# A two-layer hybrid transformer block: the second attention's work follows a written plan instead of a rule

## The chip, the cores and the metric

The kernel runs on one NeuronCore of a Trainium2 chip, as one launch. The metric is device time in microseconds (us). TensorE (PE) does the matmuls; VectorE (DVE), ScalarE (ACT) and GpSimd (POOL) do the rest of the arithmetic; SyncE (SP) issues almost all DMAs, in the order of its queue.

## The reference, cut to what matters

Two layers on 512 tokens of width 1024. The first layer's attention mixes two kinds of head; the second's has 16 heads of one kind ("moba"), and it is the one that is changed here. After each attention stands a gated feed-forward network.

```
proj = h @ w_in_odd[i]                       # h = rmsnorm(x), 512 x 1024
mq, mk, mv = jnp.split(proj, 3, axis=-1)     # 16 heads of 64 each
mq = apply_partial_rope(mq.reshape(B, S, N_MOBA_HEADS, HEAD_DIM), cos, sin)
mk = apply_partial_rope(mk.reshape(B, S, N_MOBA_HEADS, HEAD_DIM), cos, sin)
moba_out = moba_attention(mq, mk, mv)        # blocks of 256 keys, the best 3 earlier blocks and the own one
x = x + moba_out.reshape(B, S, N_MOBA_HEADS * HEAD_DIM) @ w_out_odd[i]
x = x + conv_glu_ffn(rmsnorm(x, ffn_norm[layer]), ...)
```

With 512 tokens there are two blocks, so every earlier block is always selected and the attention is plain causal attention; the kernel computes it so.

## The kernel before

All matmuls are of single-precision numbers split into a high and a low part, so a product takes three matmuls (`mm3`: high by high, low by high, high by low). A `chunk` is 128x1024 weights: SP loads it (`raw`), ACT casts its high part (`wh`), DVE subtracts the low part (`wl`). There are three buffers each of raw, wh and wl, so SP's load of a chunk waits for the `wl` of the chunk three before it, and the cast waits until PE has used the chunk three before.

The second attention handles its 16 heads as 8 pairs, p = 0 to 7, and one piece of work is one of these:

- k (`ks`): `proj` (24 matmuls of 512 columns into one of three PSUM banks "mm"), `rope` (DVE shuffle and product, POOL product, DVE sum), `halves` (ACT high part, DVE low part), and `stack_k`: six moves of 64 partitions by DMA, because the two heads of a pair need their halves at other partitions. The last two, `mk_h<-mk_h` and `mk_l<-mk_l`, wait for the moves before them.
- q (`qs`): the same with `stack_q`: `mq_a<-mq_h` and `mq_a<-mq_l` for the first head (e = 0), then `mq_l<-mq_h` for the second head (e = 1). All moves go through SP's queue, between the weight loads.
- v (`vals`): the values of two pairs at once, two chunks, 96 matmuls of 256 columns into two "mm" banks.
- s (`soft`): the scores and softmax of one head. Eight matmuls (two for each block of 128 queries) go through two PSUM banks "S" (`s_m`), DVE adds the mask and takes the maximum (`prt_m`, L348), ACT takes the exponential, POOL scales. There are two `prt` buffers.
- m (`mix`): ten transposes of the probabilities on PE (`t_m`, two banks "T"), ACT and DVE split them (`pt_m_0h`, `pt_m_0l`, ..., and `p3`, which the trace calls p), eight matmuls by the values (`o_m`) into the single bank "O", and an ACT copy (L383) and a DVE sum (L384) that empty it into `y`.
- o (`out_proj`): a quarter of the output projection for the first four pairs.

The order in which the pieces are written comes from `heads`: the scores of a head, then an equal share of the work due for the next pair, then the value products of the head before. The order inside each engine's queue is then set by the framework's scheduler, which takes the written order as priority and moves an instruction back while it takes its inputs or buffers to be not ready. No engine reorders at run time: an instruction that waits holds up all behind it on its engine.

Before any `rope` of this attention can finish, `moba_scale` must have run: it makes the row scale of the norm (`rstd_of`: four transposes `st_n`, a DVE reduction, a dozen small DVE instructions, four transposes `bc_n`) and scales the two rope tables (`CR`, `SR`). Before, it was called inside the first `v_group`, the first piece.

Of the kernel before, what the change touches and what calls it, by code (L numbers as in the profile page):

```python
# [46 lines left out]

N_BIG, N_V, N_TMP, N_COL, N_PR, N_W = 25, 2, 7, 8, 2, 3
N_PSUM = {"mm": 3, "S": 2, "T": 2, "O": 1}


def _pieces(c, bits):
# [19 lines left out]
def hybrid_kernel(ctx: ExitStack, tc: tile.TileContext, xT_d, pos_d, const_d, vec_d, w_d, out_d, idx):  # L72
    nc = tc.nc
    V, A, G, PE = nc.vector, nc.scalar, nc.gpsimd, nc.tensor
# [13 lines left out]
    def tmp(name):  # L88
        return tp.tile([P, T], F32, tag="tmp", name=name, bufs=N_TMP)
# [146 lines left out]
    def halves(y, nm, eng=V):  # L236
        h, l = big(f"{nm}_h"), big(f"{nm}_l")
        split(h, l, y, eng)
        return h, l
# [284 lines left out]
                done(2 * p + e, Q[1])  # L524
        last(Q[1])

    def heads(pairs, work):


        work = list(work)  # L530
        prev = None

        def finish(pr):
            p, e, probs = pr
            c = pairs[p]
            mix(f"{c['nm']}{e}", e, probs, values[c["v"]], c["hv"] + e, c["y"])
            if e == 1:
                c["out"].append(halves(c["y"], f"o_{c['nm']}", c.get("lo", V)))

        for p, c in enumerate(pairs):  # L540
            while work and work[0][0] <= p:
                work.pop(0)[1]()
            c["y"] = tmp(f"y_{c['nm']}")
            for e in range(2):
                probs = soft(f"{c['nm']}{e}", e, c["q"], c["k"], c["bias"], c["decay"][e] if "decay" in c else None)
                n = len([1 for w in work if w[0] <= p + 1])
                for _ in range((n + 1 - e) // (2 - e)):
                    work.pop(0)[1]()
                if prev is not None:
                    finish(prev)  # L550
                prev = (p, e, probs)
        finish(prev)
        for w in work:
            w[1]()

    values = {}

# [6 lines left out]
    w = chunk("misc", 512)  # L564
# [102 lines left out]
    def fox(p):  # L667
        def vals():
            values["f", p // 2] = v_group(f"fv{p // 2}_")

        def qs():
            c["q"] = stack_q(scaled(proj(f"fq{p}"), f"fq{p}"), f"fq{p}")

        def ks():
            c["k"] = stack_k(scaled(proj(f"fk{p}"), f"fk{p}"), f"fk{p}", G)

        c = {"nm": f"f{p}", "v": ("f", p // 2), "hv": 2 * (p % 2), "bias": causal, "out": fo, "lo": G,
             "decay": [(selr[:, P + h:P + h + 1], ck) for h in (2 * p, 2 * p + 1)]}
        return c, ([vals] if p % 2 == 0 else []) + [ks, qs]

    def dsa(p):
        def vals():
# [24 lines left out]
            c["k"] = stack_k(o, f"dk{p}")  # L707

        c = {"nm": f"d{p}", "v": ("d", p // 2), "hv": 2 * (p % 2), "bias": [causal[0]] + tmask[1:], "out": do}
        return c, [ks, qs] + ([vals] if p % 2 == 0 else [])  # L710

    pairs, work = [], []
    for n in range(8):
        c, w = (fox if n < 4 else dsa)(n % 4)
        pairs.append(c)
        if n == 0:
            w = [x for i, f in enumerate(w) for x in (f, lambda i=i: index_scores(i + 1))]
        elif n == 2:
            w.append(lambda: select(1, range(16)))
        elif n > 2 and n < 5:  # L720
            w[1:1] = [lambda n=n: select(n - 1, range(8))]
            w.append(lambda n=n: select(n - 1, range(8, 16)))
        work += [(n, f) for f in w]
        if n == 7:
            work.append((7, lambda: out_proj("oe0_", fo, part=[0])))
    work += [(8, lambda m=m: out_proj("oe0_", fo, part=[m])) for m in range(1, 4)]
    heads(pairs, work)
    acc = sq_acc(1)
    out_proj("oe1_", do, lambda d: prep(d, 1, acc))
    lo_on_pool = False  # L730
# [8 lines left out]


    def moba_scale():
        rstd_main(accs[2], "n2")
        rope_scaled()

    mo = ([], [])

    def moba(p):
        def vals():
            values["m", p // 2] = v_group(f"mv{p // 2}_", moba_scale if p == 0 else None)

        def qs():
            c["q"] = stack_q(rope(proj(f"mq{p}"), f"mq{p}"), f"mq{p}")

        def ks():
            c["k"] = stack_k(rope(proj(f"mk{p}"), f"mk{p}"), f"mk{p}")

        c = {"nm": f"m{p}", "v": ("m", p // 2), "hv": 2 * (p % 2), "bias": causal, "out": mo[p // 4]}
        return c, ([vals] if p % 2 == 0 else []) + [ks, qs]

    pairs, work = [], []  # L760
    for n in range(8):
        c, w = moba(n)
        pairs.append(c)
        work += [(n, f) for f in w]
        if n == 7:
            work.append((7, lambda: out_proj("oo0_", mo[0], part=[0])))
    work += [(8, lambda m=m: out_proj("oo0_", mo[0], part=[m])) for m in range(1, 4)]
    heads(pairs, work)
    accs[3] = sq_acc(3)
    out_proj("oo1_", mo[1], lambda d: prep(d, 3, accs[3]))  # L770
    fin = {}
# [153 lines left out]
```

## Time and profile before

| | |
|---|---|
| median of 3 runs | 1262.97 us (1261.54 to 1265.6) |
| the profiled execution, own time | 1261.51 us |
| its span, first to last instruction | 1259.7 us |
| mean granted TensorE clock | 0.993 |
| PE busy over the span | 1220.4 us, 97% |
| DVE, ACT, POOL busy | 810.9, 557.4, 357.7 us |
| the second attention in the trace | 637.11 to 885.68 us |

The stretch of the second attention begins with its first projection matmul and ends with the first matmul of the second feed-forward network. "Busy" is the union of an engine's instructions; a matmul's record is longer than its pace, so a stall shows first in the distance between two starts.

### The profile page before, as it was taken

The page shows a single profiled execution, that of the slowest core. Times are in us where ns is not written, and L with a number is a line of the kernel's source. Part 1 is how long each engine was busy: PE and PEld are TensorE (multiplying, and loading weights), DVE is VectorE, ACT ScalarE, POOL GpSimd, SP SyncE. Part 2 cuts the span into 40 slices and gives each one's busy share as a digit, 9 for nine tenths or more (in the row PEclk, how much of TensorE's full clock was granted, in tenths as well). Part 3 has the DMA queues.
Part 4 walks back from the last instruction along what each step waited for, and adds up shares of the span by engine and source line. Part 5 has one row for each costly group of instructions (what it writes and reads, how often), then busy time and mean ns, then how long its engine had stood idle before and what let it go on. Part 6 is the DMA issues. An engine that isn't in the chain of part 4 may idle for free.

```text
span 1259.7 us, 16807 instructions
## 1 busy us (share of the span) xinstructions
PE 1220.4 (97%) x5996; PEld 1018.3 (81%) x5996; DVE 810.9 (64%) x1489; ACT 557.4 (44%) x969; POOL 357.7 (28%) x394
## 2 busy tenths in 40 slices
PE   6889999999999999999999999999999999999997
PEld 4768778778888888888887888888888888888887
DVE  7889988675654555544666778787655555444555
ACT  5564667653332333333445556555433333332334
POOL 3665557542111111111213223332222111111110
PEclk9989999999999999999999999999999999999999
DMA  5333444222333322323325434331233332333321
GB/s 194 101 92 111 128 99 128 63 80 89 101 100 100 98 90 93 96 93 100 103 96 142 113 100 123 105 109 67 84 93 108 100 100 92 94 100 101 96 88 67
DMA packets 57379, 127.24 MB, mean 101 GB/s; under 512 B 7584, under 2 KB 21024, under 8 KB 57296
## 3 DMA queue, kind: packets, MB, share of 16 engines
q1 hardware_dynamic: 56368, 124.81, 33.2%
q10 hardware_dynamic: 864, 1.17, 0.3%
q8 instruction: 47, 0.77, 0.2%
q14 instruction: 36, 0.29, 0.1%
q0 software_dynamic: 64, 0.20, 0.0%
HBM read 104.13 MB, written 2.10 MB: 84 GB/s over the span
## 4 chain that ended last, share of the span: by engine, by line
PE 79%; DVE 10%; issue 5%; ACT 3%; DMA 2%; POOL 1%; POOLq 0%; ACTq 0%; DVEq 0%; SPq 0%
PE mm_g L160 6%; PE mm_g L161 6%; PE mm_g L159 6%; PE mm_u L161 6%; PE mm_u L159 6%; PE mm_u L160 6%; PE mm_d L161 6%; PE mm_d L160 6%; PE mm_d L159 6%; DVE tmask L630 2%; DVE m L629 1%; DMA mq_l<-mq_h 1%; PE t_m L372 1%; PE o_m L381 1%; PE mm_mk L160 1%
## 5 line engine op out<-in xcount | busy, mean ns | idle before, releaser
L434 POOL TENSOR_TENSOR cv<-cv,gs 128x512 f32<-128x512 f32 x44 | 57.1, 1298 | 546.2 <-ACT gs L433 546.2
L159 PE MATMUL mm_d<-a_h,wh_d 128*128 128x512 f32 (+1 forms) x384 | 142.8, 372 | 0.0
L160 PE MATMUL mm_d<-a_l,wh_d 128*128 128x512 f32 (+1 forms) x384 | 142.6, 371 | 0.0
L161 PE MATMUL mm_d<-a_h,wl_d 128*128 128x512 f32 (+1 forms) x384 | 142.6, 371 | 0.0
L503 DVE TENSOR_TENSOR us<-mm_u,cv 128x512 f32<-128x512 f32 x44 | 30.4, 692 | 168.1 <-PE mm_u L161 132.7
L160 PE MATMUL mm_g<-xl,wh_g 128*128 128x512 f32 x352 | 137.2, 390 | 0.4 <-DVE xl L175 0.4
L159 PE MATMUL mm_u<-xh,wh_u 128*128 128x512 f32 x352 | 137.3, 390 | 0.0
L161 PE MATMUL mm_u<-xh,wl_u 128*128 128x512 f32 x352 | 137.0, 389 | 0.0
L160 PE MATMUL mm_u<-xl,wh_u 128*128 128x512 f32 x352 | 137.0, 389 | 0.0
L161 PE MATMUL mm_g<-xh,wl_g 128*128 128x512 f32 x352 | 137.0, 389 | 0.0
L159 PE MATMUL mm_g<-xh,wh_g 128*128 128x512 f32 x352 | 137.0, 389 | 0.0
L148 ACT CAST wh_g<-raw_g 128x1024 fp32r<-128x1024 f32 x44 | 46.3, 1052 | 143.1 <-PE mm_g L160 141.6
L500 DVE TENSOR_TENSOR gs<-mm_g,RB 128x512 f32<-128x512 f32 x44 | 30.4, 691 | 118.2 <-PE mm_g L161 115.7
L128 ACT CAST wh_d<-raw_d 128x1024 fp32r<-128x1024 f32 x45 | 47.4, 1054 | 123.7 <-PE mm_u L160 103.4
L160 PEld LDWEIGHTS mm_d<-a_l,wh_d 128*128 128x128 f32 x384 | 72.3, 188 | 12.5
L159 PEld LDWEIGHTS mm_d<-a_h,wh_d 128*128 128x128 f32 x384 | 72.3, 188 | 12.5
L161 PEld LDWEIGHTS mm_d<-a_h,wl_d 128*128 128x128 f32 x384 | 72.3, 188 | 12.4
L160 PEld LDWEIGHTS mm_g<-xl,wh_g 128*128 128x128 f32 x352 | 66.1, 188 | 14.8 <-DVE xl L175 1.1
L161 PEld LDWEIGHTS mm_u<-xh,wl_u 128*128 128x128 f32 x352 | 66.1, 188 | 13.8
L159 PEld LDWEIGHTS mm_g<-xh,wh_g 128*128 128x128 f32 x352 | 66.1, 188 | 13.7
L161 PEld LDWEIGHTS mm_g<-xh,wl_g 128*128 128x128 f32 x352 | 66.1, 188 | 13.7
L160 PEld LDWEIGHTS mm_u<-xl,wh_u 128*128 128x128 f32 x352 | 66.1, 188 | 13.6
(778 smaller groups left out, 3072.4 us busy)
## 6 DMA issues: line engine op xcount, KB each, us to landing
raw_g<-in_w SPq DMA_DIRECT2D x44, 512.0 KB, 3.5
raw_u<-in_w SPq DMA_DIRECT2D x44, 512.0 KB, 3.6
raw_d<-in_w SPq DMA_DIRECT2D x41, 256.0 KB, 2.9
raw_d<-in_w SPq DMA_DIRECT2D x29, 192.0 KB, 2.6
raw_d<-in_w SPq DMA_DIRECT2D x34, 128.0 KB, 2.4
raw_oe<-in_w SPq DMA_DIRECT2D x8, 512.0 KB, 4.0
raw_mv<-in_w SPq DMA_DIRECT2D x8, 512.0 KB, 3.5
raw_mk<-in_w SPq DMA_DIRECT2D x8, 512.0 KB, 4.0
```

What stands on the lines that cost most here:

```text
L128: A.copy(dst_h, src)
L148: A.copy(wh, raw)
L159: PE.matmul(out, ah, bh, start=first, stop=False)
L160: PE.matmul(out, ah, bl, start=False, stop=False)
L161: PE.matmul(out, al, bh, start=False, stop=last)
L372: PE.transpose(t[:, n * P:n * P + P], probs[i][:, j * P:j * P + P], ident)
L381: PE.matmul(o[:, o0:o0 + w], vj, ph[:, c0:c0 + w], start=j == 0, stop=False)
L434: G.tensor_tensor(cv, cv, gs, op=OP.mult)
L500: V.tensor_tensor(gs, og, RB, op=OP.mult)
L503: V.tensor_tensor(us, ou, cv, op=OP.mult)
L629: V.max(m8, sc)
L630: V.match_replace(sc, m8, sc, -3e38)
```

## The change

`heads` is replaced by `attention`, which goes through a plan, a string of steps such as `k3` (keys of pair 3), `s10` (scores of pair 1, head 0) or `m10` (its value products). The first attention's plan, PLAN0, writes out the order that `heads` gave: on every engine the rows are the same as before up to the second attention. PLAN1 for the second attention is a different order. `moba_scale` now runs after the first projection of any kind, which is q of pair 1. No instruction is added or removed: PE has 5990 rows either way, DVE 1420, ACT 849, POOL 399, SP 461. Lines of the changed kernel stand 12 further down (L148 becomes L160).

```
+PLAN1 = (
+    "q1 q0 k0 k3 v0 s00 k1 q2 m00 k2 s01 s10 s11 q3 s20 q4 s21 m01 v2 m10 m11 k4 s30 s31 m20 m21 v4 k5 q6 "
+    "m30 q5 s40 m31 s41 m40 k6 s50 k7 s51 m41 v6 q7 o0 s60 s61 s70 m50 m51 s71 o1 m60 m61 o2 o3 m70 m71 "
+)
...
-    def heads(pairs, work):
...
-            c["y"] = tmp(f"y_{c['nm']}")
-            for e in range(2):
-                probs = soft(f"{c['nm']}{e}", e, c["q"], c["k"], c["bias"], c["decay"][e] if "decay" in c else None)
-                n = len([1 for w in work if w[0] <= p + 1])
-                for _ in range((n + 1 - e) // (2 - e)):
-                    work.pop(0)[1]()
-                if prev is not None:
-                    finish(prev)
-                prev = (p, e, probs)
...
+    def attention(pairs, plan, pieces):
...
+        for step in plan.split():
+            kind, n = step[0], step[1:]
+            if kind == "s":
+                c, e = pairs[int(n[0])], int(n[1])
+                if e == 0:
+                    c["y"] = tmp(f"y_{c['nm']}")
+                probs[n] = soft(f"{c['nm']}{e}", e, c["q"], c["k"], c["bias"], c["decay"][e] if "decay" in c else None)
+            elif kind == "m":
+                c, e = pairs[int(n[0])], int(n[1])
+                mix(f"{c['nm']}{e}", e, probs.pop(n), values[c["v"]], c["hv"] + e, c["y"])
...
     def moba_scale():
-        rstd_main(accs[2], "n2")
-        rope_scaled()
+
+        if 2 in accs:
+            rstd_main(accs.pop(2), "n2")
+            rope_scaled()
...
         def ks():
-            c["k"] = stack_k(rope(proj(f"mk{p}"), f"mk{p}"), f"mk{p}")
+            o = proj(f"mk{p}")
+            moba_scale()
+            c["k"] = stack_k(rope(o, f"mk{p}"), f"mk{p}")
```

On PE, the first scores of pair 2's second head (`s_m21_0`, which needs the move `mq_l` of pair 2's queries) stood in the middle of the next pair's projection `mm_mq3`, 14.6 us of matmuls behind the last one of their own projection `mm_mq2`:

```order
L159 MATMUL mm_mq3_6629<-xh_74,wh_mq3_6624 128x512
L160 MATMUL mm_mq3_6629<-xl_75,wh_mq3_6624 128x512
L161 MATMUL mm_mq3_6629<-xh_74,wl_mq3_6625 128x512
L268 MATMUL s_m21_0_6594<-mk2_bh_6311,mq2_l_6428 128x256
L269 MATMUL s_m21_0_6594<-mk2_bl_6315,mq2_l_6428 128x256
L268 MATMUL s_m21_1_6600<-mk2_bh_6311,mq2_l_6428 128x256
L269 MATMUL s_m21_1_6600<-mk2_bl_6315,mq2_l_6428 128x256
L159 MATMUL mm_mq3_6629<-xh_74,wh_mq3_6624 128x512
```

Now they stand 40.8 us of matmuls behind it, among the value products of pair 1's two heads (`o_m10`, `t_m11`), with the projection `mm_mk4` as the only filler:

```order
L281 MATMUL s_m20_3_6391<-mk2_l_6220,mq2_a_6142 128x512
L393 MATMUL o_m10_6637<-p3_0_0_94,mv0__5901 128x256
L394 MATMUL o_m10_6637<-p3_0_1_95,mv0__5901 128x256
L384 MATMUL t_m11_0_6678<-const_70,prt_m11_6295 128x128
L393 MATMUL o_m10_6637<-p3_0_0_94,mv0__5901 128x256
L280 MATMUL s_m21_0_6449<-mk2_bh_6223,mq2_l_6139 128x256
L281 MATMUL s_m21_0_6449<-mk2_bl_6227,mq2_l_6139 128x256
L384 MATMUL t_m11_0_6678<-const_70,prt_m11_6295 128x128 x3
L280 MATMUL s_m21_1_6455<-mk2_bh_6223,mq2_l_6139 128x256
L281 MATMUL s_m21_1_6455<-mk2_bl_6227,mq2_l_6139 128x256
L172 MATMUL mm_mk4_6719<-xl_75,wh_mk4_6714 128x512
L394 MATMUL o_m10_6637<-p3_0_1_95,mv0__5901 128x256
```

What moved is the scores, away from their projection and into denser company.

On DVE, the rope of pair 5's queries (`rs_mq5` is the shuffle, `mq5_l` the low part whose end lets the moves go) stood right behind the keys' rope, with two splits of probabilities inside it:

```order
L129 TENSOR_TENSOR mk5_l_7126<-ry_mk5_7120,mk5_h_7125 128x512
L225 STREAM_SHUFFLE rs_mq5_7239<-mm_mq5_7214 128x512
L226 TENSOR_TENSOR ry_mq5_7240<-mm_mq5_7214,CR_89 128x512
L129 TENSOR_TENSOR pt_m31_0l_7139<-t_m31_0_7142,pt_m31_0h_7138 128x512
L129 TENSOR_TENSOR pt_m31_1l_7141<-t_m31_1_7149,pt_m31_1h_7140 128x384
L228 TENSOR_TENSOR ry_mq5_7240<-ry_mq5_7240,rs_mq5_7239 128x512
```

Now it stands behind the softmax of pair 4's first head (`prt_m40`), a weight split (`wl_mv3`) and the split of `p3`; the scores that need it (`s_m50_0`) come 12.4 us of matmuls after the projection:

```order
L166 TENSOR_TENSOR wl_mv3_0_7540<-raw_mv3_0_7538,wh_mv3_0_7539 128x1024
L141 TENSOR_TENSOR p3_0_1_95<-t_m30_2_7132,p3_0_0_94 128x256
L360 ISA prt_m40_7197,mx_m40_1_7207<-s_m40_1_7204,cmask_83 128x256
L360 ISA mx_m40_1_7207 128x1
L141 TENSOR_TENSOR p3_0_1_95<-t_m30_2_7132,p3_0_0_94 128x128
L360 ISA prt_m40_7197,mx_m40_2_7213<-s_m40_2_7210,cmask_83 128x384
L360 ISA mx_m40_2_7213 128x1
L237 STREAM_SHUFFLE rs_mq5_7181<-mm_mq5_7156 128x512
L396 TENSOR_TENSOR y_m3_6762<-y_m3_6762,o_m30_7114 64x512
L238 TENSOR_TENSOR ry_mq5_7182<-mm_mq5_7156,CR_89 128x512
L360 ISA prt_m40_7197,mx_m40_3_7219<-s_m40_3_7216,cmask_83 128x512
```

So the queries of pair 5 are the one projection whose lead did not become long. In SP's queue, the last move of pair 1's keys (`mk1_l<-mk1_l`) had no load inside its group:

```order
L244 DMA mk1_bh_5999<-mk1_h_5995 64x512 x2
L244 DMA mk1_bl_6003<-mk1_l_5996 64x512 x2
L244 DMA mk1_h_5995<-mk1_h_5995 64x512
L244 DMA mk1_l_5996<-mk1_l_5996 64x512
L244 DMA mq1_a_6079<-mq1_h_6075 64x512
```

Now a weight load stands in front of it:

```order
L256 DMA mk1_bh_6093<-mk1_h_6089 64x512 x2
L256 DMA mk1_bl_6097<-mk1_l_6090 64x512 x2
L256 DMA mk1_h_6089<-mk1_h_6089 64x512
L159 DMA raw_mk4_6713<-in_w 128x1024
L256 DMA mk1_l_6090<-mk1_l_6090 64x512
```

That load waits for the low part of the weights of `mq4`, which waits until PE has finished `mq2`.

## Rows read from the trace of the kernel before

**Rows 1.** The page, first part: busy us (share of the span) xinstructions

```profile
PE 1220.4 (97%) x5996; PEld 1018.3 (81%) x5996; DVE 810.9 (64%) x1489; ACT 557.4 (44%) x969; POOL 357.7 (28%) x394
```

**Rows 2.** Stretches: us; busy PE, PEld, DVE, ACT, POOL; PE clock; DMA share, GB/s

```profile
400.00:637.11 237.11, 237.11 (x1048) 196.39 (x1046) 126.10 (x152) 81.18 (x98) 41.89 (x33) 1.00 0.31 98
637.11:885.68 248.57, 242.58 (x1385) 207.72 (x1384) 188.02 (x400) 136.09 (x296) 70.06 (x86) 1.00 0.37 105
```

**Rows 3.** Waits of PE from 637 to 886: total us, times, longest

```profile
PE s_m L268 <- DMA mq_l<-mq_h: 3.3, 3, 1.3
PE s_m L268 <- DMA mq_a<-mq_l: 1.0, 1, 1.0
PE o_m L381 <- ACT pt_m_0h L128: 0.8, 4, 0.2
PE bc_n L204 <- DVE y_n L201: 0.6, 1, 0.6
```

**Rows 4.** Timeline of PE at the score waits: start, us, what, [idle before]

```profile
670.67 0.36 PE L268 MATMUL s_m<-mk_h,mq_a 128*128 128x256 f32 x1 [0.98 <-DMA mq_a<-mq_l]
...
675.93 0.36 PE L268 MATMUL s_m<-mk_bh,mq_l 128*128 128x256 f32 x1 [1.35 <-DMA mq_l<-mq_h]
...
720.56 0.39 PE L160 MATMUL mm_mq<-xl,wh_mq 128*128 128x512 f32 x1
720.78 0.39 PE L161 MATMUL mm_mq<-xh,wl_mq 128*128 128x512 f32 x1
722.39 0.36 PE L268 MATMUL s_m<-mk_bh,mq_l 128*128 128x256 f32 x1 [1.22 <-DMA mq_l<-mq_h]
...
772.78 0.36 PE L268 MATMUL s_m<-mk_bh,mq_l 128*128 128x256 f32 x1 [0.72 <-DMA mq_l<-mq_h]
```

**Rows 5.** Timeline of SP's issues for the queries of pair 2

```profile
713.89 0.46 SPq L244 DMA_DIRECT2D mq_a<-mq_l  x1
...
716.80 0.33 SPq L147 DMA_DIRECT2D raw_mk<-in_w  x1
717.19 0.47 SPq L244 DMA_DIRECT2D mq_l<-mq_h  x1
```

**Rows 6.** Chain that ended last (start, us, what); landings of tiles `mq_a`, then `mk_l`

```profile
642.84 1.06 ACT wh_mq L148
...
666.09 4.44 DMA mq_a<-mq_l
...
717.19 5.07 DMA mq_l<-mq_h
...
DMA to landing us min/median/max: 2.2/2.2/4.6
...
DMA to landing us min/median/max: 2.2/2.9/4.8
```

**Rows 7.** Timelines of DVE and SP: shuffles (q 0, k 1, q 2) and a last move

```profile
660.89 0.74 DVE L225 STREAM_SHUFFLE rs_mq<-mm_mq 128x512 f32<-128x512 f32 x1
666.33 0.74 DVE L225 STREAM_SHUFFLE rs_mk<-mm_mk 128x512 f32<-128x512 f32 x1
705.82 0.74 DVE L225 STREAM_SHUFFLE rs_mq<-mm_mq 128x512 f32<-128x512 f32 x1
...
677.16 0.54 SPq L244 DMA_DIRECT2D mk_l<-mk_l  x1
```

**Rows 8.** Timeline of PE: transposes of the first head, and of the second

```profile
677.87 1.31 PE L372 MATMUL t_m<-const,prt_m 128*128 128x128 f32 x5
...
698.67 0.93 PE L372 MATMUL t_m<-const,prt_m 128*128 128x128 f32 x7
```

**Rows 9.** Bank "O" emptied: last product on PE, sum on DVE (L384)

```profile
708.51 0.28 PE L382 MATMUL o_m<-p,mv__5681 128*128 128x256 f32 x1
...
709.44 0.68 DVE L384 TENSOR_TENSOR y_m<-y_m,o_m 64x512 f32<-64x512 f32 x1 [0.41 <-ACT y_m L383]
```

**Rows 10.** Weight splits on DVE: count, ns min/median/max, first and last start

```profile
L154 DVE TENSOR_TENSOR wl_mq<-raw_mq,wh_mq x8: 1225/1605/1979, 643.9 to 801.3; 128x1024 fp32r<-128x1024 f32 x8
```

More of the change, by code (lines that the diff above doesn't have):

```diff
@@ L49 @@
 N_PSUM = {"mm": 3, "S": 2, "T": 2, "O": 1}
+PLAN0 = (
[3 rows of a table added]
+)
+PLAN1 = (
+    "q1 q0 k0 k3 v0 s00 k1 q2 m00 k2 s01 s10 s11 q3 s20 q4 s21 m01 v2 m10 m11 k4 s30 s31 m20 m21 v4 k5 q6 "
+    "m30 q5 s40 m31 s41 m40 k6 s50 k7 s51 m41 v6 q7 o0 s60 s61 s70 m50 m51 s71 o1 m60 m61 o2 o3 m70 m71 "
+)
 def _pieces(c, bits):
@@ L525, in ffn @@
         last(Q[1])
-    def heads(pairs, work):
[L530 to L541, printed above, removed]
-                work.pop(0)[1]()
-            c["y"] = tmp(f"y_{c['nm']}")
-            for e in range(2):
-                probs = soft(f"{c['nm']}{e}", e, c["q"], c["k"], c["bias"], c["decay"][e] if "decay" in c else None)
-                n = len([1 for w in work if w[0] <= p + 1])
-                for _ in range((n + 1 - e) // (2 - e)):
-                    work.pop(0)[1]()
-                if prev is not None:
-                    finish(prev)
-                prev = (p, e, probs)
-        finish(prev)
-        for w in work:
-            w[1]()
+    def attention(pairs, plan, pieces):
+        probs = {}
+        for step in plan.split():
[8 more added lines that the diff above has]
+                mix(f"{c['nm']}{e}", e, probs.pop(n), values[c["v"]], c["hv"] + e, c["y"])
+                if e == 1:
+                    c["out"].append(halves(c["y"], f"o_{c['nm']}", c.get("lo", V)))
+            else:
+                pieces[kind](int(n))
     values = {}
@@ L678, in fox @@
              "decay": [(selr[:, P + h:P + h + 1], ck) for h in (2 * p, 2 * p + 1)]}
-        return c, ([vals] if p % 2 == 0 else []) + [ks, qs]
+        return c, ks, qs, vals
     def dsa(p):
@@ L709, in dsa, with attend @@
         c = {"nm": f"d{p}", "v": ("d", p // 2), "hv": 2 * (p % 2), "bias": [causal[0]] + tmask[1:], "out": do}
[L710 to L727, printed above, removed]
+        return c, ks, qs, vals
+    def attend(made, plan, **pieces):
+        for k, n in (("k", 1), ("q", 2), ("v", 3)):
+            pieces[k] = lambda p, n=n: made[p][n]()
+        attention([m[0] for m in made], plan, pieces)
+    attend([fox(p) for p in range(4)] + [dsa(p) for p in range(4)], PLAN0,
+           i=index_scores, x=lambda n: select(n // 10, range(n % 10 * 4, n % 10 * 4 + 4)),
+           o=lambda m: out_proj("oe0_", fo, part=[m]))
     acc = sq_acc(1)
@@ L748, in vals @@
         def vals():
-            values["m", p // 2] = v_group(f"mv{p // 2}_", moba_scale if p == 0 else None)
+            values["m", p // 2] = v_group(f"mv{p // 2}_", moba_scale)
         def qs():
-            c["q"] = stack_q(rope(proj(f"mq{p}"), f"mq{p}"), f"mq{p}")
+            o = proj(f"mq{p}")
+            moba_scale()
+            c["q"] = stack_q(rope(o, f"mq{p}"), f"mq{p}")
         def ks():
-            c["k"] = stack_k(rope(proj(f"mk{p}"), f"mk{p}"), f"mk{p}")
+            o = proj(f"mk{p}")
+            moba_scale()
+            c["k"] = stack_k(rope(o, f"mk{p}"), f"mk{p}")
         c = {"nm": f"m{p}", "v": ("m", p // 2), "hv": 2 * (p % 2), "bias": causal, "out": mo[p // 4]}
[L758 to L768, printed above, removed]
+        return c, ks, qs, vals
+    attend([moba(p) for p in range(8)], PLAN1, o=lambda m: out_proj("oo0_", mo[0], part=[m]))
     accs[3] = sq_acc(3)
```

3 rows, old and new, of the table PLAN0 are left out of this document.

## The prediction

> **What bounds the kernel now.** I read the page first: PE is busy 97% of the span [rows 1], so the time is PE's work plus its stalls. Then busy time by stretch: in the feed-forward network before, PE is busy for 237.11 of 237.11 us; in the second attention for 242.58 of 248.57, with the granted clock at 1.00 (the 2.4 GHz level), so its stalls cost no clock [rows 2]. All that an order can win in the part that moves is thus some 6 us of visible idle time. DVE, the next engine, is busy 188.02 of 248.57 us: no bound on the average, though it can be one locally.
>
> Third, the waits of PE in that stretch [rows 3]: scores wait for the moves of the queries, 3.3 us in three places and 1.0 us in one; the first value product of a head waits for ACT's split in four, 0.8 us together; `bc_n` waits 0.6 us.
>
> Fourth, the four score waits in time [rows 4]. A 512-column matmul starts 0.22 us after the one before it (720.56, 720.78; 0.23 on most). From 720.78 to 722.39 pass 1.61 us, so this wait costs 1.38, or 0.16 more than the idle time shown, since a matmul's record is longer than its pace. The idle times add to 4.27 us; with 0.16 each the four waits cost **4.9 us**. PE works in order and hardly idles elsewhere, so this is time of the kernel.
>
> Why were those moves late? For pair 2 the shuffle began on DVE at 705.82 [rows 7]. `mq_a`'s second half was issued at 713.89; SP then went through weight loads, the last at 716.80, before it issued the move `mq_l` at 717.19 [rows 5], which took 5.07 us to land, where the moves to `mq_a` take 2.2 in the median [rows 6]. That is 16.4 us from shuffle to landing, and the order gave it 14.6 us of matmuls.
>
> **The change part by part.** Every engine has the same instructions as before, so only waits change. I count leads in the two orders as PE time between two places: the matmuls between, at the paces above (half as long for 256 columns).
>
> *The four score waits.* From projection to first use, q of pair 0 now has 21.9 us for the first head and 40.4 for the second (8.8 and 12.2 before); the second heads of pairs 2 and 4 have 40.8 and 65.8 (14.6 each). The chain of pair 2 needed 16.4. All four waits go: **-4.9 us**, unless other chains become the short ones. Three of the new leads are near a chain's length: k of pair 0 (16.4 us), k of pair 1 (15.6), q of pair 5 (12.4).
>
> *Keys of pairs 0 and 1.* Before, pair 1's keys took from the shuffle at 666.33 to the issue of their last move at 677.16 [rows 7] 10.8 us, and 2.9 to land [rows 6]: 13.7, or 15.6 with the longest landing, 4.8. A new thing stands in SP's queue ahead of that move, the load of `mk4`. It waits for the split of `mq4`'s weights, which waits for the end of `mq2`: 5.5 us of matmuls after `mk1`, then a cast of 1.06 [rows 6] and a split of up to 1.98 [rows 10], some 9 us with what DVE has ahead of it. The move itself would not go before 10.8. I put **0**; bounds 0 and 1.
>
> *Queries of pair 5.* Before, from the shuffle to the landing of `mq_a`, pair 0 took 660.89 to 670.53 (666.09 + 4.44), 9.6 us; pair 2 took 713.89 - 705.82 + 2.2 = 10.3, or 12.7 with the longest landing, 4.6 [rows 5 to 7]. In the new order the shuffle stands behind softmax work whose scores come up to 1.8 us after the projection, so I let it start 2.4 us into the 12.4; 10.0 remain for 9.6 to 12.7. A wait of 0 to 2.7; pair 2's row gives 0.3, and I take **+0.6**, since the start can only slip later.
>
> *The start.* `bc_n` stands 9.9 instead of 9.7 us into the stretch, but the chain of small DVE instructions that it waits for now has a shuffle of 0.74 us [rows 7] ahead of its reduction: **+0.3**; bounds 0 and 0.7. q1 and q0 occupy two of three "mm" banks until the rope tables are scaled, and `mk3` needs one back at 17.2 us. That is hidden by the projections of q0 and k0, 11 us; with only one of them, 5.5 us would be missing.
>
> *The first head's transposes.* Five took 1.31 us where seven of the second head took 0.93 [rows 8], because they came 3.5 us after the scores. They now have 9.5: **-0.5**; bounds -0.6 and 0.
>
> *The bank "O".* Emptying it takes from the last product's start to the end of the sum, 708.51 to 710.12, 1.6 us [rows 9]. Before, the next head's first product came 3.4 us later at the least. Now those of pairs 1 and 2 come after 1.8 and 2.1 us, that of pair 5 after 2.5; and for pair 1 a weight split of 1.23 to 1.98 us [rows 10] stands on DVE ahead of the sum. I take **+0.7** in all; bounds 0 and 3 (a slow split ahead of each of three sums, less the slack and ACT's copy that runs beside it). Behind a late sum the splits of the next head wait, and PE's products for them.
>
> *Other waits of dense places* (`o_m` for ACT, 0.8 us [rows 3]): **0**. By my count DVE's work comes to some 19.5 us in the densest 20 us of matmuls, against 18 before. Bounds -0.8 and, for five such places at 2 us, +10; I stay near nothing, since the old order had such places too and its rows show 0.2 us each.
>
> **Sum:** -4.9 + 0.6 + 0.3 - 0.5 + 0.7 = **-3.8 us**. The profiled execution took 1261.51 us (span 1259.7), so it would take 1257.7. The median of the runs lies 1.46 above it: 1262.97 - 3.8 = **1259.2 us**. What a measurement of this kernel can tell from no change is about 0.3%, 3.8 us. The forecast sits on that line.
>
> **The rivals.**
>
> 1. *Moves behind loads eat the gain.* A move queued behind two loads landed in 5.07 us, not 2.2. If that holds where the new order puts loads ahead of a move that is needed soon, k1 and q5 take their upper bounds, 1 and 2.7 us, instead of 0 and 0.6: -3.8 + 3.1 = -0.7; with the bank at its bound, +1.6. Some 1262.3 to 1264.6, and with part of it **1261.5**, no change that can be told. For it: the 4.44 and 5.07 in the chain [rows 6]. Against it: the median landings are 2.2 and 2.9.
>  The Trainium skill, "DMA: Bandwidth & Descriptors", section "Queues, rings and completion order", states the rule behind this: a DMA engine takes the descriptors of one ring in ring order, so a move on SP's queue goes behind the load. The rows agree where a load is just ahead.
> 2. *Nothing new waits.* The four score waits and the first head's go, 5.4 us, and no new one comes; `o_m` may save up to 0.8 more: **1257.0**. For it: the leads are two to four times as long. Against it: leads do not help `o_m`, which waits for its own transposes.
> 3. *Slower: the dense places become bound by DVE.* In five places two heads' softmax and two heads' products interleave (m10 to s21, m20 to s31, s40 to m41, m50 to s61, m60 to s71). A slow weight split of 1.98 us ahead of a sum or split that PE needs costs up to 2 us in each: +10 - 5.4 = +4.6, **1267.6**. It decides from (5.4 + 3.8)/5 = 1.85 us in each place. For it: the count of DVE's work; against it: the 0.2 us above.
>  The Trainium skill, "SBUF — State Buffer", section "SBUF: two separate sides", says that a DVE instruction with two SBUF inputs and a POOL instruction that reads SBUF exclude each other while either runs. The spread of the splits, 1.23 to 1.98, is in line with that, though less than POOL's whole instruction.
> 4. *The change does nothing*, because the scheduler restores its own order: the rows of the orders exclude it.
>
> **How the numbers follow.** The forecast's case (gain of 2.5 to 5 us) has 0.45, rival 1 0.30, rival 2 0.17, rival 3 0.08. The 0.3% line cuts the forecast's case a little above its middle, so it gives 0.28 to faster and 0.17 to the same; of rival 1, 0.04 is given to faster, since one of its two moves may keep its time, and 0.26 to the same. Faster 0.28 + 0.04 + 0.17 = 0.49, the same 0.43, slower 0.08. The range leaves about one in ten on each side: from 1256.0, past most of rival 2, to 1263.5, inside rival 1.
>
> **What would show it.** Right: in the profile after, the second attention lasts some 245 us; PE's waits of `s_m` for `mq_l` and `mq_a` are gone but for one of under 1 us at pair 5's first scores; `bc_n` waits 0.6 to 1.2 us; and the first products of the second heads of pairs 1 and 2 wait some tenths. Wrong: score waits of 1 us or more for `mk_l`, waits of PE for DVE or ACT of over 5 us in all, or a time that changes outside this attention.

## The result, and the profile after

| | before | after |
|---|---|---|
| median of 6 runs | 1262.74 us (1261.54 to 1266.08) | 1254.11 us (1253.63 to 1254.98) |
| ratio, 95% interval | | 0.9926 (0.9912 to 0.994) |
| profiled execution, span | 1261.51, 1259.7 us | 1253.63, 1251.9 us |
| second attention in the trace | 637.11 to 885.68, 248.57 us | 636.19 to 876.91, 240.72 us |

The changed kernel is faster by 8.6 us. The forecast was 3.8 us, and the time lies 1.9 us below the range. The stretch that was changed gives 7.85 us of it, so the place was right and the size was not.

From the page after, busy time by engine, beside [rows 1]:

```profile
PE 1215.0 (97%) x5996; PEld 1014.6 (81%) x5996; DVE 812.9 (65%) x1489; ACT 556.2 (44%) x969; POOL 359.3 (29%) x394
```

By stretch, as in [rows 2] (us; busy PE, PEld, DVE, ACT, POOL; PE clock; DMA share, GB/s):

```profile
400.00:636.19 236.19, 236.19 (x1043) 195.57 (x1042) 125.89 (x152) 80.71 (x98) 41.93 (x32) 1.00 0.33 98
636.19:876.91 240.72, 239.79 (x1386) 206.69 (x1384) 189.29 (x400) 134.78 (x296) 70.49 (x86) 1.00 0.39 108
```

Of 6.0 us in which PE was not busy in the second attention, 0.9 are left, and its busy time fell by 2.8 us with the same instructions, since a matmul that is held up has a longer record (the first scores of pair 2's second head: 0.36 us in [rows 4], 0.28 below). These are all waits of PE that the view lists there, beside [rows 3]:

```profile
PE t_m L384 <- DVE pt_m_0l L141: 0.5, 2, 0.4
PE bc_n L216 <- DVE y_n L213: 0.3, 1, 0.3
```

Every score wait is gone, and so are the four listed waits of value products for ACT. Timeline of PE after, at the places of which the prediction spoke (start, us, what, [idle before]):

```profile
646.69 0.51 PE L216 MATMUL bc_n<-const,y_n 128*128 128x128 f32 x3 [0.35 <-DVE y_n L213]
...
682.73 0.93 PE L384 MATMUL t_m<-const,prt_m 128*128 128x128 f32 x7
...
724.83 0.28 PE L280 MATMUL s_m<-mk_bh,mq_l 128*128 128x256 f32 x1
...
727.75 0.39 PE L393 MATMUL o_m<-pt_m_0h,mv__5901 128*128 128x512 f32 x1
...
782.01 0.28 PE L280 MATMUL s_m<-mk_h,mq_a 128*128 128x256 f32 x1
```

In order: `bc_n`; the first head's transposes, now with the pace of [rows 8]'s second row; the first scores of pair 2's second head, which [rows 4] show with a wait of 1.22; the first product of pair 1's second head into bank "O"; the first scores of pair 5. Only `bc_n` waits. The last had 2.4 us to spare, as SP's issues of pair 5's moves and the landing of these moves show:

```profile
776.58 0.46 SPq L256 DMA_DIRECT2D mq_a<-mq_h  x1
777.37 0.46 SPq L256 DMA_DIRECT2D mq_a<-mq_l  x1
...
DMA to landing us min/median/max: 2.2/2.2/2.2
```

777.37 + 2.2 = 779.57, against a use at 782.01.

To put a size on every kind of wait, I took the distance between the starts of each two neighbouring matmuls in the stretch, less the pace of the first (0.227 us for 512 columns, 0.171 for 384, 0.114 for 256, 0.108 for a transpose), and added them up by what follows what. The sum falls from 15.84 to 7.98 us, which is the whole gain of the stretch:

| term | forecast | in the two traces |
|---|---|---|
| scores behind a projection | -4.9 | 5.25 to 0.32, -4.93 |
| transposes behind transposes | -0.5 | 0.85 to 0.27, -0.58 |
| `bc_n` | +0.3 | 0.77 to 0.51, -0.26 |
| queries of pair 5 | +0.6 | 0 |
| bank "O" | +0.7 | 0 |
| all the others | 0 | -2.09 |
| of it, products behind a projection | | 2.30 to 0.72, -1.58 |
| sum | -3.8 | -7.86 |

The two kinds of error weigh nearly the same: 1.6 us of new waits that did not come (`bc_n` even fell by 0.3), and 2.1 us of old ones, put at 0, that went.

### The profile page after: what moved, and what is told of

It is laid out like the page before. It is cut to its first block, busy times and chain, and to the rows that moved or that the text cites. A ratio compares the mean times of both kernels' runs of the same rounds, so it can differ in the third digit from the quotient of the medians.

```text
span 1251.9 us, 16800 instructions
## 1 busy us (share of the span) xinstructions
PE 1215.0 (97%) x5996; PEld 1014.6 (81%) x5996; DVE 812.9 (65%) x1489; ACT 556.2 (44%) x969; POOL 359.3 (29%) x394
## 4 chain that ended last, share of the span: by engine, by line
PE 81%; DVE 9%; issue 4%; ACT 2%; DMA 2%; POOL 2%; POOLq 0%; SPq 0%; ACTq 0%; DVEq 0%
PE mm_g L172 6%; PE mm_g L173 6%; PE mm_g L171 6%; PE mm_u L172 6%; PE mm_u L171 6%; PE mm_u L173 6%; PE mm_d L172 6%; PE mm_d L171 6%; PE mm_d L173 6%; DVE tmask L632 2%; DVE m L631 1%; PE t_m L384 1%; PE mm_mk L171 1%; PE mm_mk L173 1%; PE mm_mq L173 1%
## 5 line engine op out<-in xcount | busy, mean ns | idle before, releaser
L160 ACT CAST wh_g<-raw_g 128x1024 fp32r<-128x1024 f32 x44 | 46.3, 1052 | 143.2 <-PE mm_g L172 141.6
L172 PEld LDWEIGHTS mm_d<-a_l,wh_d 128*128 128x128 f32 x384 | 72.3, 188 | 12.4
L171 PEld LDWEIGHTS mm_u<-xh,wh_u 128*128 128x128 f32 x352 | 66.1, 188 | 13.7
```

The lines of the kernel that those rows point to most:

```text
L160: A.copy(wh, raw)
L171: PE.matmul(out, ah, bh, start=first, stop=False)
L172: PE.matmul(out, ah, bl, start=False, stop=False)
```

## The experiments

What is changed is the second attention's plan unless said otherwise. The stage column is the stretch from its first projection matmul to the first matmul of the second feed-forward network, read from PE's timeline. It tells more than the whole time does: in the profiled executions with an unchanged first attention (e6, which changes buffers, aside) the stage began anywhere between 635.07 and 639.07, while three with the changed kernel's plan (it and b1, b2 below) took 240.72, 240.49 and 240.69. "One" and "two" are the heads by which the plan writes the value products behind the scores; where they come to stand is up to the scheduler.

| run | projections | products behind scores, as written | ratio to before, 95% | stage, us |
|---|---|---|---|---|
| before | old | one | 1 | 248.57 |
| e3 | old | two | 1.0008 (0.9993 to 1.0024) | 249.44 |
| e2 | one pair ahead | one | 0.9968 (0.9952 to 0.9983) | 245.49 |
| e12 | one pair ahead | two | 0.9953 (0.9936 to 0.9969) | 243.77 |
| e7 | as changed | one | 0.9976 (0.9966 to 0.9986) | 246.02 |
| after | as changed | two | 0.9926 (0.9912 to 0.994) | 240.72 |
| e8 | as changed, but opening v0 k0 q0 k1 q1 | two | 0.9934 (0.9919 to 0.9949) | 241.65 |
| e4 | old, new opening | one | 1.0011 (0.9998 to 1.0024) | 249.77 |
| e5 | old, no moves of queries | one | 0.9981 (0.997 to 0.9993) | 246.52 |

**The parts of the plan.** Theory A: late moves, and what they set off, are all of the gain. Theory B: the moves are worth 4.9 us, and the rest is the place of the value products.

e2, every projection one pair of heads earlier:

```diff
-"v0 k0 q0 s00 k1 s01 q1 m00 s10 v2 k2 m01 s11 q2 m10 s20 k3 m11 s21 ...
+"v0 k0 q0 k1 q1 s00 k2 s01 q2 m00 s10 v2 k3 m01 s11 q3 m10 s20 k4 m11 s21 ...
```

> The order of before with every projection written one pair of heads earlier, and the value products one head behind the scores as before; values first, as before. Theory A (the lead of the moves is all): the gain of the changed kernel nearly in full, 7 to 8.5 us, ratio 0.9935. Theory B (moves 4.9 us, the rest from the place of the value products): 5 to 5.5 us, ratio 0.996, with TensorE's waits of value products for ScalarE left at 0.8 us or more.

4.0 us less by the ratio, nearest to B. PE's waits in the stage:

```profile
PE s_m L280 <- DVE mx_m L360: 1.7, 2, 1.3
PE o_m L393 <- ACT pt_m_0h L140: 0.7, 3, 0.3
PE bc_n L216 <- DVE y_n L213: 0.6, 1, 0.6
```

No score waits for a move any more, but scores now wait for a bank "S" that DVE's maximum gives back late: of the 4.9 us the stage keeps 3.1. The value products did not gain by the leads: counted from start to start, they lose 2.89 us behind projections, against 2.30 in before.

e3, products written two heads behind, projections as before:

```diff
-"v0 k0 q0 s00 k1 s01 q1 m00 s10 v2 k2 m01 s11 q2 m10 s20 ...
+"v0 k0 q0 s00 k1 s01 q1 s10 m00 v2 k2 s11 m01 q2 s20 m10 ...
```

> The order of before with the value products written two heads behind the scores and the projections where they were. Theory A: the score waits for the moves stay at 3 to 5 us, ratio 0.999 to 1.001. Theory B: the waits for moves stay, the other 2 to 3 us go: ratio 0.998. If two heads behind is what matters most, 0.995 or less.

No change, but this is no test of the spacing, because the scheduler put the products back. On PE the scores and value products of the 16 heads begin in exactly the sequence of before, and 1245 of the stage's 1384 matmuls stand in the same order: the first product of pair 1's first head, for instance, starts at 713.23, ahead of pair 2's first scores at 716.3, as in before (714.00, 716.76). The moves stay late (3.4 us of waits for `mq_l` and `mq_a`).

e4, the opening alone:

```diff
-"v0 k0 q0 s00 k1 s01 q1 m00 s10 ...
+"q1 q0 k0 v0 s00 k1 s01 m00 s10 ...
```

> The order of before but for its opening: queries of pairs 1 and 0 first, then keys 0 and values. Theory A and B alike: the two score waits of pair 0 (2.3 us idle, 2.6 us of pace) and half a microsecond of the first transposes go, the two later ones stay: 2.5 to 3.5 us less, ratio 0.9975. If the opening is what was underrated, 5 us or more.

A miss for every theory. PE's waits in the stage:

```profile
PE s_m L280 <- DMA mq_l<-mq_h: 2.3, 2, 1.5
PE t_m L384 <- POOL prt_m L365: 1.7, 3, 0.9
PE s_m L280 <- ACT mv__5852 L418: 0.9, 1, 0.9
...
PE s_m L281 <- DMA mk_l<-mk_l: 0.6, 1, 0.6
```

The two waits of the first pair's queries went, and the first scores and transposes then waited for other engines instead.

e5 takes the moves of the queries away and leaves the old places:

```diff
         h, l = halves(y, nm)
+        if nm[0] == 'm':
+            return h, h
```

> The written order of before, but the scores of the second attention read the projected queries where they lie: the three moves of each query projection are left out (so its scores are not the reference's). That takes all four waits for moves away with the old places kept. Theory A (late moves and what they set off are all of the gain): 7.5 to 8.5 us less than before, ratio 0.9935. Theory B (the moves cost 4.9 us, the rest comes from where the new order puts the value products): 4.5 to 5.5 us less, ratio 0.996, with the value products' waits for ScalarE left at 0.7 us or more.

2.4 us less, below both. The waits that replace the moves:

```profile
PE o_m L395 <- ACT pt_m_0h L140: 1.0, 3, 0.6
PE t_m L386 <- POOL prt_m L367: 0.8, 2, 0.5
PE s_m L282 <- DMA mk_h<-mk_h: 0.6, 1, 0.6
```

The scheduler also brought the scores forward here: 251 of PE's 1384 matmuls stand elsewhere than in before. With e2 it says the same: with the products written one head behind, taking 4.9 us of score waits away is worth 2 to 3 us of stage.

e7 has the changed kernel's projections with the products one head behind. e8 has its plan, but begins with the values, keys and queries of pair 0 as before did, with pair 1's projections still ahead of the first scores:

```diff
-"q1 q0 k0 k3 v0 s00 k1 q2 m00 k2 s01 s10 s11 q3 s20 q4 s21 m01 v2 m10 m11 k4 ...
+"q1 q0 k0 k3 v0 s00 k1 q2 s01 m00 k2 s10 m01 s11 q3 m10 s20 q4 m11 s21 v2 m20 k4 ...   (e7)
+"v0 k0 q0 k1 q1 s00 k2 q2 m00 k3 s01 s10 s11 q3 s20 q4 s21 m01 v2 m10 m11 k4 ...       (e8)
```

> The changed kernel's plan with its projections in their places, but the value products one head behind the scores, as before. Theory A (the lead is all): as the changed kernel, 8 to 8.6 us less than before, ratio 0.9932. Theory B (the place of the value products is worth some 2.7 us): 5 to 6 us less, ratio 0.9957, with waits of value products for ScalarE of 0.7 us or more.

> The changed kernel's plan with the opening of before: values, keys 0, queries 0, keys 1, queries 1, then scores. If the opening is worth little once the rest is ahead: 7 to 8.5 us less than before, ratio 0.994. If the opening carries the first pair's two waits: these come back, 2.6 us, ratio 0.9955.

e7 keeps 3.0 us, less than either theory gave it; e8 keeps the gain but for 0.9 us of stage, so queries first or values first matters little. The written place of the products is worth 5.3 us of stage with the changed kernel's projections. With e2's it is worth 1.7 (e2 against e12), so the 5.3 belong to this plan and not to the spacing alone. e12 puts the same two ideas on e2's places:

```diff
-"v0 k0 q0 k1 q1 s00 k2 s01 q2 m00 s10 v2 k3 m01 s11 q3 m10 s20 k4 m11 s21 ...
+"v0 k0 q0 k1 q1 s00 k2 q2 s01 m00 k3 s10 s11 q3 m01 s20 k4 s21 m10 v2 m11 ...
```

> The plan with each projection one pair of heads earlier than before and values first (4.1 us less than before), now with the value products two heads behind the scores: the two ideas of the change without its own sequence. If the two ideas together are the gain: 7.5 to 8.5 us less, ratio 0.9936. If the changed kernel's own sequence is needed: as without it, 4 to 5 us less, ratio 0.9965.

It lies between the two expectations: the ideas together give 4.8 us of stage, the changed kernel's own sequence another 3.

**Why one head behind loses 5 us.** PE's two largest kinds of wait in e7, and the four engines at the longest of them (first the waits, then timelines of DVE, POOL, ACT and PE):

```profile
PE o_m L393 <- ACT pt_m_0h L140: 1.6, 3, 1.1
PE s_m L280 <- DVE mx_m L360: 0.9, 2, 0.6
```

```profile
716.59 0.74 DVE L237 STREAM_SHUFFLE rs_mq<-mm_mq 128x512 f32<-128x512 f32 x1
...
716.83 2.06 POOL L365 TENSOR_SCALAR prt_m<-prt_m,sm_m 128x128 f32<-128x128 f32 x4 [5.04 <-DVE sm_m L363]
718.86 1.30 POOL L239 TENSOR_TENSOR rs_mq<-rs_mq,SR 128x512 f32<-128x512 f32 x1
...
720.19 0.69 DVE L240 TENSOR_TENSOR ry_mq<-ry_mq,rs_mq 128x512 f32<-128x512 f32 x1 [1.17 <-POOL rs_mq L239]
...
720.92 0.62 ACT L140 CAST mq_h<-ry_mq 128x512 fp32r<-128x512 f32 x1 [3.21 <-DVE ry_mq L240]
721.56 0.58 ACT L140 CAST pt_m_0h<-t_m 128x512 fp32r<-128x512 f32 x1
...
722.20 0.50 PE L393 MATMUL o_m<-pt_m_0h,mv__5901 128*128 128x512 f32 x1 [1.10 <-ACT pt_m_0h L140]
```

Read from the end: the value product waits for the split of its probabilities, whose transposes had ended at 717.4; the split stands on ACT behind the high part of a projection of queries, before which ACT is idle for 3.21 us; that waits for the rope's sum on DVE, the sum for POOL's product, and the product stands on POOL behind the softmax scaling of the head just scored. Two theories: C, this chain is what costs; D, DVE is simply too full where softmax and splits fall together.

e9, the high parts of projections on POOL, and e10, the low parts of the weights on POOL, both on e7's plan:

```diff
-        split(h, l, y, eng)
+        G.tensor_copy(h, y)
+        V.tensor_tensor(l, y, h.bitcast(F32), op=OP.subtract)      (e9, names that begin with m)
...
+    lo_on_pool = True                                             (e10, ahead of the second attention)
```

> The plan of the run with value products one head behind (3.0 us less than before), with one edit: the high part of each projection is made on GpSimd instead of ScalarE. In that run ScalarE stood idle for 2 to 3 us before two such casts, waiting for VectorE's rope, with the split of the next probabilities queued behind, and TensorE waited 1.6 us for it. Theory C (one head behind loses because the splits stand behind the high parts on ScalarE): the waits of value products fall from 1.6 us to some 0.5, and about 1.5 us come back: ratio 0.9965 or a little under. Theory D (it loses because VectorE is too dense where softmax and splits fall together): no gain, 0.9976 as without the edit.

> The same plan, one head behind, with the low parts of the second attention's weights made on GpSimd (four instructions of some 0.8 us each for a chunk) instead of VectorE (1.6 us a chunk): some 38 us less work on VectorE in the stage. Theory D (VectorE's density is what one head behind runs into): the waits of scores for VectorE's maximum (0.9 us) and of value products go, ratio 0.995 or less. Theory C: the rope is a little earlier, 0.5 to 1 us, ratio 0.997. If the later low parts (3.2 us a chunk) hold up the projections, slower than without the edit.

e9: ratio 1.000 (0.9987 to 1.0014), stage 249.55. The waits of products fell from 1.6 to 0.2 us as C said, but DVE now waited for POOL's copy before the low parts of the projections (5.9 us in all before `mq_l`, as much before `mk_l`), and what stood behind them on DVE was late:

```profile
PE t_m L388 <- DVE pt_m_0l L141: 3.3, 3, 1.3
PE s_m L284 <- DVE mx_m L364: 2.0, 4, 0.7
```

e10: 1.008 (1.005 to 1.011), stage 262.26, with 6.0 us of scores waiting for DVE's maximum. Neither tells C from D; both loaded POOL.

e13 takes work off DVE and puts none elsewhere (PE reads the high part of the weights in place of the low one), e14 takes the product of the rope off POOL, e15 puts that product on DVE, all on e7's plan:

```diff
         A.copy(wh, raw)
+        if low_out:
+            return wh, wh                                          (e13, second attention)
...
-        G.tensor_tensor(s, s, SR, op=OP.mult)
+        if nm[0] != 'm' or nm == 'misc':                           (e14: left out in the second attention)
+            G.tensor_tensor(s, s, SR, op=OP.mult)
...
+        (V if nm[:2] in ('mq', 'mk') else G).tensor_tensor(s, s, SR, op=OP.mult)      (e15)
```

> The plan with value products one head behind (3.0 us less than before), with the low parts of the second attention's weights left out: TensorE reads the high part in their place (so the output is not the reference's), and VectorE has 24 to 32 instructions of some 1.4 us less in the stage, with no work put on another engine. Theory D (one head behind runs into VectorE): most of the 5 us between it and the changed kernel come back, ratio 0.994 or less. Theory C (the chain of a projection across GpSimd and ScalarE stands ahead of the splits, whatever VectorE's load): 1 us or so, ratio 0.997.

> The same plan, one head behind, with GpSimd's product of the rope left out (so the scores are not the reference's); TensorE's order is the same row for row. In the run without the edit, GpSimd took the rope of a query projection behind the softmax scaling of the head just scored, VectorE's sum waited for it, ScalarE's cast for the sum, and the split of the next probabilities stood behind that cast: TensorE waited 1.1 us. Theory C: the waits of value products go from 1.6 us to 0.5 or less, 1 to 2 us come back, ratio 0.9965. Theory D: VectorE's queue is late anyway, no difference, 0.9976.

> The plan with value products one head behind (3.0 us less than before), with the product of the rope made on VectorE instead of GpSimd: nothing is left out, VectorE has 16 instructions of some 0.7 us more, and the rope no longer passes GpSimd's queue, where it stood behind the softmax scaling. Theory C: the waits of value products fall from 1.6 us to some 0.5, and 1 to 2.4 us come back, ratio 0.996. Theory D (the load of VectorE): slower than without the edit, 0.998 to 1.001.

e13: 1.0006 (0.9991 to 1.002), stage 247.82. PE's waits:

```profile
PE o_m L400 <- ACT pt_m_0h L140: 2.8, 3, 1.8
PE s_m L287 <- DVE mx_m L367: 2.0, 4, 0.6
```

DVE was busy for 155.25 us instead of e7's 187.62, and nothing was won. That speaks against D without excluding it, since the scheduler's order is another one: 501 of PE's 1384 matmuls stand elsewhere than in e7. e14: 0.9957 (0.9941 to 0.9972), stage 243.08, with the order of e7 on PE, DVE and ACT; the waits for DVE's maximum are gone and PE's are down to

```profile
PE bc_n L216 <- DVE y_n L213: 0.3, 1, 0.3
PE s_m L281 <- DMA mk_h<-mk_h: 0.3, 1, 0.3
PE o_m L394 <- ACT p L140: 0.2, 1, 0.2
PE o_m L394 <- ACT pt_m_0h L140: 0.2, 1, 0.2
```

e15: 0.9947 (0.9933 to 0.996), stage 243.13, with nothing left out and DVE given more (columns as in [rows 2]):

```profile
637.33:880.46 243.13, 241.71 (x1385) 206.74 (x1384) 191.06 (x416) 136.10 (x296) 54.10 (x70) 1.00 0.39 107
```

DVE is busy for 3.4 us more than in e7 and the stage is 2.9 us shorter, so D falls by this run. C is borne out for these 2.9 of the 5.3 us: counted from start to start, products lose 1.05 us behind projections instead of 3.12. The chain is shortened, not gone: in e15, too, ACT is idle for 3.36 us before the same cast, but the split ends 0.8 us earlier and the product waits for 0.1 us. One rival is not excluded: without POOL's product DVE's weight splits are shorter as well (last section), 39.8 us in e14 and 40.3 in e15 where e7 has 45.4. In the chain shown it plays no part, for the one weight split on DVE there (715.16) took 1.22 us, the time of one alone; for the rest of the 2.9 us no run separates the two. Of the other 2.4 us, 0.7 is a wait of scores for DVE's maximum in e15; the rest lies in many small pieces, and what causes them no run tells.

**Other runs.** e1 kept before's order and issued the move `mq_l` from POOL's queue:

```diff
-        move(l[LO], h[HI])
+        move(l[LO], h[HI], nc.gpsimd if 'm' == nm[0] else None)
```

> The order of before, but the last move of each query projection of the second attention (the one that the second head's scores wait for) is issued from GpSimd's queue instead of SyncE's. No piece moves. Theory A (late moves, and the waits that they set off behind them on ScalarE and VectorE, are all of the gain): the three waits for that move, 3.8 us, go and take about 2 us of other waits of TensorE with them: some 6 us less than before, ratio 0.9955. Theory B (the moves cost 4.9 us and no more, the other 3 us of the gain come from where the new order puts the value products): 3.8 us less, ratio 0.997, and the waits of the value products for ScalarE stay at 0.8 us. Under both the wait for the first head's queries (1.0 us) stays.

1.0054 (1.0035 to 1.0072), stage 253.67: slower, and no test of A and B, since the three waits for the move stay (PE resumes 0.1 us after each landing, though the view names DVE or issue there). For pair 2 the place in the queue was not what held the move, which was issued here:

```profile
721.61 0.55 POOL L256 DMA_DIRECT2D mq_l<-mq_h  x1 [0.91 <-DMA mq_a<-mq_l]
```

It overwrites what the move before it (`mq_a<-mq_l`) reads, so it waits for that one to land. On SP's queue it does so too, in five of eight cases in before (view of SP's waits there):

```profile
SPq L244 <- DMA mq_a<-mq_l: 5.9, 5, 1.9
```

For pair 2, 3.3 us lay between the issues of these two moves in before (713.89 to 717.19); 2.2 of them are that landing, and 1.1 the weight load in SP's queue. In e1 it is 2.7 us. On POOL's queue the move still took 4.5 us to land. Of the 5.1 us by which the stage grew, 3.5 lie at transposes behind a projection, which wait for POOL's scaling (2.4 us idle).

e6 gave before a fourth buffer for high parts of weights and took two large activation buffers for it:

```diff
-N_BIG, ... = 25, ...
+N_BIG, ... = 23, ...
...
-bufs=N_W
+bufs=N_W + (t == 'wh')
```

> The order of before with four instead of three buffers for the high parts of the weights (and 23 instead of 25 of the large activation buffers, to make room). In the trace of before the first value product of a head waits where ScalarE has a weight cast ahead of the split of the probabilities, and that cast waits until TensorE gives a weight buffer back. Theory B1 (these waits come from the cast): the waits at a projection of values and at the last output projections go, 1 to 1.5 us in all, ratio 0.999; the waits for moves stay. Theory A: they are set off by the late moves, which stay: no difference in them, ratio 1.000.

1.0088 (1.0067 to 1.0109): the stage began 9.2 us later, and in it (251.11 us) the products' waits for ACT stayed at 0.8 us. B1 is not borne out; the lost activation buffers may hide what the fourth buffer gave. Nor did it clear the way on ACT: the split stands behind a weight cast that waits for PE as in before, only that of the next chunk:

```profile
737.15 1.05 ACT L160 CAST wh_mq<-raw_mq 128x1024 fp32r<-128x1024 f32 x1 [2.29 <-PE mm_mq L172]
738.23 0.59 ACT L140 CAST pt_m_0h<-t_m 128x512 fp32r<-128x512 f32 x1
```

b1 and b2 kept the second attention's new plan and tried the two ideas in the first, where PE's waits are longer:

```diff
-"v0 i1 k0 i2 q0 i3 s00 k1 s01 q1 m00 s10 ...
+"v0 i1 k0 i2 q0 i3 k1 s00 q1 s01 m00 s10 ...                           (b1)
+"v0 i1 k0 i2 q0 i3 k1 q1 s00 k2 s01 x10 x11 m00 q2 s10 x12 x13 ...      (b2)
```

> The changed kernel with two moves in the first attention's plan as well: keys of pair 1 ahead of the first scores, the rest one place further; the last selection of keys ahead of the values of pair 4. If leads pay in the first attention as in the second: the wait of the first scores for their queries (3.4 us) goes, 2 to 4 us less than the changed kernel, ratio to before 0.991. If what was covered by that wait is late next: the same as the changed kernel, 0.993.

> The changed kernel with the first attention written by the same two ideas: every projection one pair of heads ahead, value products two heads behind. If the two ideas carry over: 4 to 6 us less than the changed kernel, ratio to before 0.989. If VectorE, which also selects keys there, is the bound: no gain or slower, 0.993 to 0.998.

0.9995 (0.9985 to 1.0005) and 0.9961 (0.9949 to 0.9974). The second attention began at 644.84 and 639.03 instead of 636.19, and kept its 240.5 and 240.7 us: the first attention took all that was lost. In b1 its waits for moves grew from 4.0 to 8.9 us:

```profile
PE s_f L279 <- DMA fq_a<-fq_l: 4.7, 2, 3.0
PE s_d L279 <- DMA dq_a<-dq_l: 4.2, 2, 2.7
```

e11 and e16 are the changed kernel with e9's and with e15's edit.

> The changed kernel with the high part of each projection made on GpSimd instead of ScalarE. Theory C: the changed kernel's remaining waits of value products (0.7 us of pace) shrink a little: 8.5 to 9.5 us less than before, ratio 0.9928. Theory D: as the changed kernel, 0.9932. The lead of the moves shortens by the slower cast; if a lead was near its limit, waits for moves come back.

> The changed kernel with the same edit. Its value products wait for little, so theory C expects little: 8.5 to 9.5 us less than before, ratio 0.9928. If the work added to VectorE is felt: 0.994 to 0.996.

0.9943 (0.9927 to 0.996), stage 241.68, and 0.9938 (0.9924 to 0.9952), stage 240.67: no gain on top, as expected if the chain that costs one head behind its time is covered in the changed plan (in e16 the scheduler also moved 287 of PE's 1384 matmuls). No version tried beats the changed kernel's ratio.

## Why the prediction was wrong

- *Four score waits, -4.9.* Right in the trace, -4.93, and by the step given: leads of 22 to 66 us. (Of the 3.3 us that pair 2's move stood back in SP's queue, the loads that the working names made only 1.1; see e1.) But the size holds only with the rest of the plan. With the products written one head behind (e2, e5) the same waits leave and 2 to 3 us of others come. That a stall had given DVE, ACT and POOL time to catch up is my reading, not shown by a run.
- *Other waits of dense places, 0.* This step failed: -2.09 in the traces, -1.58 of it value products behind a projection, where the lower bound was -0.8. It was mis-sized from the start, by taking idle time for cost: priced from start to start, as the score waits were, the four waits of [rows 3] cost 1.41 us, and two more that the view does not list 0.49. Of the reason given ("leads do not help `o_m`, which waits for its own transposes") the first half holds, as e2 shows; the second is wrong. ACT before, and PE, at one of [rows 3]'s four waits (timelines):

```profile
725.69 1.05 ACT L148 CAST wh_mk<-raw_mk 128x1024 fp32r<-128x1024 f32 x1 [3.00 <-PE mm_mq L160]
726.76 0.59 ACT L128 CAST pt_m_0h<-t_m 128x512 fp32r<-128x512 f32 x1
...
727.40 0.50 PE L381 MATMUL o_m<-pt_m_0h,mv__5681 128*128 128x512 f32 x1 [0.17 <-ACT pt_m_0h L128]
```

The transposes had ended at 719.1. The split began 7.6 us later, behind a weight cast that itself waited 3.0 us for PE; at two of the four waits it stands so, at the other two behind the softmax's exponentials on ACT. Which instruction stands ahead on ACT is a matter of the whole order, and the new order changes it. I had counted the softmax and the products of two heads in one place as a risk (rival 3, DVE-bound); e7 and e15 show the opposite sign: the plan that is written one head behind is the one that collides, and not through DVE's load.
- *Queries of pair 5, +0.6.* Did not come. From shuffle (772.6) to landing (779.57) they took 7.0 us, not 9.6 to 12.7: no load stood just ahead of the moves, which landed in 2.2 us. The shuffle itself began 3.8 us after the projection's last matmul, later than the 2.4 that I had allowed.
- *Bank "O", +0.7.* Did not come: the sum of pair 1's first head ran from 726.84 to 727.52 on DVE, and the next product started at 727.75, 0.2 us behind it. The slack was as short as forecast, but the weight split ahead of the sum took 1.22 us and not the longest 1.98. The 3.4 us "at the least" of before was misread, too: before its very last head there are 2.05 us, and no wait.
- *Start, +0.3.* `bc_n` cost 0.3 us less instead of 0.3 more. *Keys, 0,* and *transposes, -0.5,* were right.
- *The rivals.* The second, nothing new waits (1257.0), was nearest and still 2.9 us short, because it, too, let the old small waits stand. Of the first, moves behind loads, no wait is left, although after still has an `mq_l` that took 4.6 us to land: the leads cover it. Its reason is open besides, since in e1 five of the eight moves took 4.4 to 5.3 us on POOL's queue as well, and so did not need a load ahead of them in their own queue to be slow. The step that made the forecast too small is thus the sum over places: three of its terms were new waits taken at a middle value although each had a bound of 0, and all the small waits that were there already were taken to stay.

## What to carry to other kernels

A wait that is read as "for ACT" or "for DVE" is often one for whatever stands ahead in that engine's queue: look at what the releasing engine did just before, and whether its own inputs had long been there. Removing one stall in a kernel where all engines are coupled through in-order queues need not pay its full price: here leads alone gave 3 of 8 us (e2), the whole plan all of them, and the spacing alone could not be had, because the scheduler undid it (e3). So look at the order that came out, too, before you read what a plan was worth. Where many small waits stand in a stage that is reordered as a whole, put a range around them on the gain side too.

## What the hardware showed

Making the low part of a weight chunk on DVE (128x1024, both inputs in SBUF) takes 1.21 to 1.23 us in all 17 cases after where POOL ran nothing beside it. With POOL's product of the rope beside it, it takes 1.96 to 2.31, in nine cases, in all of which POOL's product had begun first (timelines of DVE and POOL after):

```profile
678.73 2.31 DVE L166 TENSOR_TENSOR wl_mq<-raw_mq,wh_mq 128x1024 fp32r<-128x1024 f32 x1
...
678.68 1.29 POOL L239 TENSOR_TENSOR rs_mk<-rs_mk,SR 128x512 f32<-128x512 f32 x1
```

POOL's product keeps its 1.3 us. In e14, which has no such product, the weight splits of the keys are uniform (the tile `wl_mk`, ns min/median/max, after and e14):

```profile
L166 DVE TENSOR_TENSOR wl_mk<-raw_mk,wh_mk x8: 1211/1610/2055, 637.3 to 764.0; 128x1024 fp32r<-128x1024 f32 x8
```

```profile
L166 DVE TENSOR_TENSOR wl_mk<-raw_mk,wh_mk x8: 1211/1218/1235, 638.0 to 768.8; 128x1024 fp32r<-128x1024 f32 x8
```

This is the spread of [rows 10], now with its cause. In e10, with POOL full of two-input products, DVE's rope sum took 1.34 us in the mean (keys) where e7's took 0.70, while the split of probabilities, whose input lies in PSUM, kept 0.69. The Trainium skill, "SBUF — State Buffer", section "SBUF: two separate sides", says that a DVE instruction with two SBUF inputs and a POOL instruction that reads SBUF hold the shared port in turn, each for its whole length. For POOL's products the trace agrees (1.22 + 1.29 = 2.51 would be the most). For POOL's softmax scaling it agrees as well, but there it is mostly POOL that waits. Beside it the four weight splits after took 1.21 to 1.31 us, while the four scalings of a head, 2.06 us in e7's timeline above, took 3.03 with the weight split of 676.33 beside them (timeline of POOL after):

```profile
675.68 3.03 POOL L365 TENSOR_SCALAR prt_m<-prt_m,sm_m 128x128 f32<-128x128 f32 x4 [12.47 <-DVE sm_m L363]
```

In a few cases the split waited instead: in e15 two such splits took 1.58 and 1.59 us.
